# Norm 1 with common roots and weights spread by TensorE, the first projections in chunks of 256 in a fixed order, and the last pair's factors later

## The chip, the core and the metric

The kernel runs on one core of one Trainium2 chip. The metric is device time in microseconds (us) from one execution of the program to its end; the median of several runs is compared. Engines are named as the profile names them: PE is TensorE (PEld its weight loads), DVE is VectorE, ACT is ScalarE, POOL is GpSimd, SP is SyncE, which here only issues DMAs.

## What is computed

One inference step of a hybrid decoder layer for 1024 new tokens of one sequence and 8 sample tokens, 1032 rows in all, of width 1024, in fp32:

```python
h = rms_norm(x, norm1_g)                       # x * rsqrt(mean(x*x) + eps) * g
q_a, k_a, v_a, q_b, k_b, v_b, o_b, i_b, f_b, g_a, g_b = split(h @ w_in)
for g in range(3):                             # windows 128, 512, 2048; dilations 1, 4, 16
    o[g], lse[g] = dilated_attention(q_a[g], k_a[g], v_a[g], bias[g])   # 8 heads of 64
a_out = sum_g(softmax_g(lse) * o)              # factors across the three groups
hm, C, n, m = mlstm(silu(conv(q_b, k_b)), v_b, i_b, f_b)
x = x + (sig(g_a) * (a_out @ w_pa) + sig(g_b) * (sig(o_b) * hm) @ w_pb) @ w_o
x = x + conv_ffn(rms_norm(x, norm2_g)); y = rms_norm(x, final_norm_g)
```

The 8 sample tokens attend to cached keys and values instead. New keys, values and states are outputs too.

## The kernel before

**Matmuls in three passes.** Every fp32 operand is split into a high part (a cast to the matmul's format) and a low part (the rest): high by high, low activation by high weight, high activation by low weight. `mm` (L207) issues for one chunk of tokens and 128 output columns 3 passes of 8 matmuls, one for each 128 of the 1024 inputs. The 1032 rows lie in three chunks, `CHUNKS` = 352, 352 and 328 columns. A weight of 128 columns comes by SP into one of 3 raw buffers (`raw_w`, L158), ACT casts the high part (`whi`, L200), DVE subtracts for the low part (`wlo`, L201), after which the raw buffer is free. Chunks go to one of 3 PSUM buffers (`pp`), which ACT or DVE empties; other PSUM results (`X`, L98) share 5 buffers. SBUF tiles of one row width come from a pool of 16 (`A`, L90).

**Norm 1.** Nine tiles of rows (`xn0` to `xn8`, the last with 8 rows). `norm1_a` (L239): ACT squares the tile and sums it into a column of `ss` (L242), DVE makes mean plus eps (L243), ACT takes the root (L244). `norm1_b`: DVE inverts, does one Newton step (L249 to L252) and scales the tile by root and weights, `gbc`, the 1024 weights that a DMA spread over all partitions (L253). `norm1_c`: PE transposes the tile in 8 pieces into two PSUM tiles (`pxt`, L262), ACT casts the high part `act_hi` (L265). `norm1_d`: DVE subtracts for `act_lo` (L271). The loop at L289 pipelines these by one tile and splits the first three weights (query, key, value of the first unit) after tiles 1, 2 and 3. These ACT and DVE instructions are kept in the order of the program (`in_order`); PE's place is left to a scheduler. The work for the tables follows: `e4` (L300), `gT` (L306), the bias products `pv` (L317) with their copies to DRAM (`vec_d`, `rep_d`), from which POOL later loads the bias tiles `bt`.

**Units.** Each of 4 pairs of heads by 3 groups is a unit. Unit 0 is computed alone (L1013): for each chunk its query, key and value are projected (L383 ff.), and then come the key and value transposes, `ptr` (L411). From there `weave` (L938) runs a unit's attention between the projections of the next one: at step i it advances the generators that a dictionary names for i, then projects one chunk. `Ahead` (L178) loads and splits the weights before they are needed.

**The last pair.** After unit 11 a last weave (L1035) does six gate chunks (`gate_steps`, which write `tga_d`) and in between three generators of pair 3. `cb` (`combine_b`) makes the factors across groups on DVE (`fw` L586 to L598, `ff` L601), transposes them on PE (`pst`, L604) and writes `f_d` (L607). `cc` (`combine_c`) loads for each group the spread factors `fbc` (L618) and the outputs `ob` (L619) on POOL, multiplies (L628), adds (L633) and writes `aT_d`. `sa` (`sample_steps`) is the sample attention: the new rows `sn` go to DRAM (`sn_d`) and come back spread (`qb`, POOL), DVE multiplies and sums with cached keys `kt` (L671, L672), PE transposes these scores (`psc`, L688) behind a bias product (`psb`, L683); SP loads cached values `vt` (L680); then come the softmax (L693 to L697), the values' products (`pos`, L721), the output `asT` (L731) and its write. After the weave `conv_in` (L1059 to L1076) follows for column blocks of the mLSTM: a projection, its evacuation to `u` on ACT (L1063), the conv on DVE (`z`, L1071 and L1073), a tanh on ACT (L1075).

**Queues.** Each engine does its instructions in the order in which they stand, and SP and POOL issue their DMAs so too: one that waits holds those behind it.

## Time and profile before

| | us |
|---|---|
| median of 3 runs (2298.34 to 2299.7) | 2298.75 |
| the profiled execution | 2297.91 |
| its span from first to last instruction | 2295.9 |
| TensorE busy in it | 2260.7 |
| VectorE busy | 1152.2 |
| ScalarE busy | 688.4 |

Rows below come from the profiled execution, with times from the start of its span; 2.0 us lie around the span. Busy time of TensorE is a model of pipelined instructions; the start of the next group is the better mark of a group's end. The thing to read in a timeline's row is, beside its start, the bracket: how long the engine was idle before it, and what ended that.

### The profile page before, as it was taken

What the parts mean: (1) busy time and instruction counts of PE and PEld (TensorE: products, weight loads), DVE (VectorE), ACT (ScalarE), POOL (GpSimd) and SP (SyncE); (2) the same over time, 40 slices, a digit from 0 to 9 for tenths busy, and PEclk for the clock granted to TensorE, in tenths of its full rate; (3) what the DMA queues carried; (4) which work ended last, traced back from release to release, by engine and by line L of the source; (5) the groups of instructions that cost most, each with busy time, mean ns of one, the idle gap of its engine ahead of it and who ended that gap; (6) DMA issues with size and microseconds to landing.
All of it is one profiled execution on the core that took longest, in us unless ns stands there. A gap on an engine that the chain in (4) does not pass through costs nothing.

```text
span 2295.9 us, 36432 instructions
## 1 busy us (share of the span) xinstructions
PE 2260.7 (98%) x15077; PEld 2170.6 (95%) x15077; DVE 1152.2 (50%) x2680; ACT 688.4 (30%) x1346; POOL 224.5 (10%) x404
## 2 busy tenths in 40 slices
PE   6999999999989999999999999999999999999998
PEld 6899999999989999999999999999999999999997
DVE  6243544444354545556332444446655656655666
ACT  4233343343323333333222311332222222221222
POOL 1112121121220111111122100000000000000000
PEclk8999999999999999999999999999999999999999
DMA  5324453545571232414245521221111111111112
GB/s 179 98 67 116 118 122 109 143 120 136 139 229 52 80 104 67 132 57 124 79 127 173 172 60 47 79 74 56 56 38 47 46 38 56 56 55 38 47 38 78
DMA packets 246471, 209.38 MB, mean 91 GB/s; under 512 B 24777, under 2 KB 220473, under 8 KB 246290
## 3 DMA queue, kind: packets, MB, share of 16 engines
q1 hardware_dynamic: 206577, 124.65, 18.8%
q0 software_dynamic: 39728, 82.42, 11.9%
q8 instruction: 118, 1.93, 0.4%
q14 instruction: 48, 0.39, 0.1%
HBM read 166.59 MB, written 45.50 MB: 92 GB/s over the span
## 4 chain that ended last, share of the span: by engine, by line
PE 95%; DVE 1%; issue 1%; DMA 1%; ACT 1%; SPq 0%; POOL 0%; DVEq 0%; ACTq 0%; POOLq 0%
PE pp L213 71%; PE ppd L1553 11%; PE s L481 2%; PE pt L508 1%; PE po L535 1%; PE pcm L1170 1%; PE ni L1164 1%; PE ptr L411 1%; PE na L1167 1%; PE sm L1151 1%; PE pxo L1421 1%; SPq L102 0%; PE pkm L1140 0%; DMA xn<-in_x_prompt_dram 0%; PE pn L1274 0%
## 5 line engine op out<-in xcount | busy, mean ns | idle before, releaser
L213 PE MATMUL pp<-act_hi,whi 128*128 128x352 f32 (+1 forms) x3272 | 600.1, 324 | 2.3 <-ACT act_hi L265 2.0
L213 PE MATMUL pp<-act_lo,whi 128*128 128x352 f32 (+1 forms) x3272 | 582.0, 320 | 0.0
L213 PE MATMUL pp<-act_hi,wlo 128*128 128x352 f32 (+1 forms) x3272 | 579.6, 319 | 0.0
L213 PEld LDWEIGHTS pp<-act_hi,whi 128*128 128x128 f32 x3272 | 524.1, 188 | 13.2 <-issue 6.3
L213 PEld LDWEIGHTS pp<-act_lo,whi 128*128 128x128 f32 x3272 | 526.1, 187 | 1.6
L213 PEld LDWEIGHTS pp<-act_hi,wlo 128*128 128x128 f32 x3272 | 525.4, 187 | 1.6
L201 DVE TENSOR_TENSOR wlo<-wraw,whi 128x1024 fp32r<-128x1024 f32 (+2 forms) x153 | 181.9, 1189 | 370.4 <-PE pp L213 206.0
L200 ACT CAST whi<-wraw 128x1024 fp32r<-128x1024 f32 (+2 forms) x153 | 156.5, 1023 | 512.1 <-PE pp L213 457.4
L1554 DVE TENSOR_TENSOR x<-x,ppd 128x352 f32<-128x352 f32 (+4 forms) x248 | 124.6, 515 | 72.4 <-PE ppd L1553 72.3
L1479 DVE TENSOR_TENSOR fu<-pp,sq 128x320 f32<-128x320 f32 (+1 forms) x130 | 64.6, 511 | 182.2 <-PE pp L213 181.9
L1553 PE MATMUL ppd<-fhi,dhi 128*128 128x352 f32 (+3 forms) x528 | 123.7, 320 | 0.2
L1553 PE MATMUL ppd<-fhi,dlo 128*128 128x352 f32 (+3 forms) x528 | 123.9, 320 | 0.0
L1553 PE MATMUL ppd<-flo,dhi 128*128 128x352 f32 (+3 forms) x528 | 123.3, 319 | 0.0
L1493 DVE SCALAR_TENSOR_TENSOR y<-fu,fcv,y 128x1048 f32<-128x1048 f32 x88 | 115.1, 1307 | 2.4 <-ACT y L1491 1.2
L495 ACT ACTIVATE sb<-sb,st 128x128 f32<-128x128 f32 (+1 forms) x192 | 84.2, 440 | 41.0 <-DVE st L490 41.0
L1553 PEld LDWEIGHTS ppd<-fhi,dhi 128*128 128x128 f32 x528 | 89.5, 188 | 1.9 <-issue 0.5
L1553 PEld LDWEIGHTS ppd<-fhi,dlo 128*128 128x128 f32 x528 | 89.5, 188 | 1.4
L1553 PEld LDWEIGHTS ppd<-flo,dhi 128*128 128x128 f32 x528 | 89.5, 188 | 1.4
L105 POOL DMA_DIRECT2D gfin<-in_final_norm_g_dram x1 | 0.5, 527 | 912.8 <-DVE fu L1479 912.8
L374 DVE COPY vT<-pp 128x352 f32<-128x352 f32 (+1 forms) x36 | 18.5, 513 | 111.3 <-PE pp L213 111.3
L490 DVE CUSTOM_DVE_ANT_0 sb<-s,bt 128x128 f32<-128x128 f32 (+1 forms) x192 | 55.5, 348 | 29.5 <-PE s L481 23.6
L1491 ACT ACTIVATE y<-fu,fcv 128x1048 f32<-128x1048 f32 x44 | 55.7, 1266 | 30.6 <-DVE fu L1481 30.3
(382 smaller groups left out, 2319.4 us busy)
## 6 DMA issues: line engine op xcount, KB each, us to landing
wraw<-in_w_in_dram SPq DMA_DIRECT2D x84, 512.0 KB
wraw<-in_w_up_dram SPq DMA_DIRECT2D x44, 512.0 KB
draw<-in_w_down_dram SPq DMA_DIRECT2D x22, 512.0 KB
c<-in_state_mlstm_C_dram SPq DMA_DIRECT2D x32, 256.0 KB
out_dram<-c POOLq DMA_DIRECT2D x32, 256.0 KB, 3.4
o_d<-oT POOLq DMA_DIRECT2D x12, 512.0 KB, 6.5
kt<-in_cache_kv_w_dram SPq DMA_DIRECT2D x12, 512.0 KB
qb<-sn_d POOLq DMA_DIRECT2D x12, 512.0 KB, 4.7
```

What stands on the lines that cost most here:

```text
L200: a = nc.scalar.copy(hi[:, 0:n], raw[:, 0:n])
L201: b = nc.vector.tensor_tensor(out=lo[:, 0:n], in0=raw[:, 0:n], in1=hi[:, 0:n].bitcast(F32), op=ALU.subtract)
L213: nc.tensor.matmul(ps[0:m, 0:n], wt[:, i * m:(i + 1) * m], act[i][which][:, t0:t0 + n], start=(pi == 0 and i == 0), stop=(pi == 2 and i == ...
L411: nc.tensor.transpose(pt[:, i * 128:(i + 1) * 128], src[:, b * 128:(b + 1) * 128], ident)
L481: yield nc.tensor.matmul(ss_[hd][:, at[b]:at[b] + kw], qT[pr, b * 128:(b + 1) * 128], kT[pr, k0 * 128:k0 * 128 + kw], start=True, stop=True)
L490: red = nc.vector.tensor_tensor_reduce(out=sb[:, 0:kw], in0=ss_[hd][:, at[b]:at[b] + kw], in1=bias[hd][:, 256 - kw:256], scale=1.0, scalar ...
L495: in_order(nc.scalar.activation(out=sb[:, 0:kw], in_=sb[:, 0:kw], func=ACTF.Exp, scale=-1.0, bias=st[:, cm:cm + 1], accum_out=st[:, cl:cl ...
L1479: nc.vector.tensor_tensor(out=u[:, 2 + t0:2 + t0 + npm], in0=ps[:, 0:npm], in1=r2[:, t0:t0 + npm], op=ALU.mult)
L1491: nc.scalar.activation(out=y, in_=u[:, 0:YW], func=ACTF.Identity, scale=fcv3[:, 0, j:j + 1], bias=fcv3[:, 3, j:j + 1])
L1493: nc.vector.scalar_tensor_tensor(out=y, in0=u[:, i:i + YW], scalar=fcv3[:, i, j:j + 1], in1=y, op0=ALU.mult, op1=ALU.add)
L1553: nc.tensor.matmul(ps[:, 0:n], wds[j][w][:, m * 128:(m + 1) * 128], parts[j][a][:, t0:t0 + n], start=(x == 0), stop=(x == len(seq) - 1))
L1554: nc.vector.tensor_tensor(out=x1[m][:, t0:t0 + n], in0=x1[m][:, t0:t0 + n], in1=ps[:, 0:n], op=ALU.add)
```

## The change

- `gbc` is no longer spread by a DMA. A row of 1024 weights is loaded (`grow`), and PE multiplies a column of ones by it, twice 512 columns in fp32 (`pgb`); ACT copies the results to `gbc`.
- Norm 1 is cut into `squares` (ACT), `stats` (root and Newton step for a list of tiles at once, in columns of `ss`), `scale` (DVE), `turn` (PE transposes and ACT casts) and `rest` (DVE low parts). Roots are taken for tiles 0, 1, (2, 3), (4, 5) and (6, 7, 8).
- Unit 0 goes by `FIRST`, chunks of 256, 256, 256 and 264. Its matmuls and the transposes are kept in program order, and the program interleaves them: `next(u0)` projects one of query, key and value of one chunk; transposes, scalings and weight splits stand between.
- The tables' work (`e4`, `gT`, bias products, `rbx`) moves to a function `tables`, called after the key projection of the third chunk. The load of the second weight moves ahead of `xn4`.
- In the last weave the steps of `sa`, `cb` and `cc` get other places: `cb` ends at step 5, all of `cc` comes after the weave.

```diff
+FIRST = ((0, 256), (256, 256), (512, 256), (768, 264))
-    gbc = A("gbc")
-    dma_w(gbc[:, 0:DM], _bcast(norm1_g, 0, [[0, 128], [1, DM]]))
+    grow = A("grow")
+    dma_w(grow[0:1, 0:DM], norm1_g[0:1, :])
...
+    gbc = A("gbc")
+    for k0 in (0, 512):
+        pgb = X("pgb")
+        in_order(nc.tensor.matmul(pgb, ones[0:1, :], grow[0:1, k0:k0 + 512], start=True, stop=True))
+        nc.scalar.copy(gbc[:, k0:k0 + 512], pgb)
...
+    def stats(tiles):
+
+        c = slice(tiles[0], tiles[-1] + 1)
+        v, r, t = (ss[:, k + c.start:k + c.stop] for k in (16, 25, 34))
+        o(nc.vector.tensor_scalar(out=v, in0=ss[:, c], scalar1=1.0 / DM, scalar2=EPS, op0=ALU.mult, op1=ALU.add))
         o(nc.scalar.activation(out=t, in_=v, func=ACTF.Sqrt))
...
     raws = [raw_w(w_in2[:, 0:128])]
     load_x(3)
+    raws.append(raw_w(w_in2[:, AQ:AQ + 128]))
     load_x(4)
-    raws.append(raw_w(w_in2[:, AQ:AQ + 128]))
     raws.append(raw_w(w_in2[:, 2 * AQ:2 * AQ + 128]))
...
+    squares(0)
+    stats((0,))
+    squares(1)
+    scale(0)
+    turn(0)
+    stats((1,))
+    squares(2)
+    scale(1)
+    rest(0)
+    turn(1)
+    squares(3)
+    first_split()
+    rest(1)
+    stats((2, 3))
+    scale(2)
...
-                for ci in range(len(CHUNKS)):
+                for ci in range(len(FIRST)):
                     for k in range(3):
-                        proj_chunk(first_w[k], hT, evacs[k], ci)
+                        proj_chunk(first_w[k], hT, evacs[k], ci, chunks=FIRST, pin=True)
                         yield
...
-    for _ in units[0].steps():
+
+    u0 = units[0].steps()
+    next(u0)
+    turn(2)
+    scale(3)
+    rest(2)
+    first_split()
+    next(u0)
+    turn(3)
+    squares(4)
+    squares(5)
+    rest(3)
+    stats((4, 5))
+    scale(4)
+    first_split()
+    next(u0)
+    turn(4)
+    scale(5)
+    rest(4)
+    next(u0)
+    turn(5)
+    for i in (6, 7, 8):
+        squares(i)
+    rest(5)
+    stats((6, 7, 8))
+    scale(6)
+    next(u0)
+    turn(6)
...
+    next(u0)
+    e4, gT = tables()
+    for _ in u0:
...
     weave(None, gate_steps(tga_d, (2, 3)), 6, {
-        0: (sa, cb, sa, sa), 1: (cb, sa), 2: (cb, sa), 3: (cb, sa, sa), 4: (sa, cc), 5: (sa, sa, cc),
+        0: (cb, sa, sa), 1: (sa,), 2: (sa,), 3: (cb, sa), 4: (cb, sa, sa), 5: (cb, sa, sa),
```

How the rows of an engine move is shown at two places. The first is ScalarE in the head. In these rows `junk,ss<-xn` is a square, `rst<-rst` or `ss<-ss` a root, `act_hi<-pxt` the casts of a transposed tile, `whi<-wraw` the cast of a weight and `qT<-pp` or `kT<-pp` the evacuation of a projection. Before:

```order
L242 ACTIVATE junk_110,ss<-xn_101 128x1024
L244 ACTIVATE rst<-rst 128x1
L242 ACTIVATE junk_111,ss<-xn_106 128x1024
L244 ACTIVATE rst<-rst 128x1
L265 CAST act_hi<-pxt 128x4x128 x2
L242 ACTIVATE junk_110,ss<-xn_108 128x1024
L244 ACTIVATE rst<-rst 128x1
L265 CAST act_hi<-pxt 128x4x128 x2
L200 CAST whi<-wraw 128x1024
L242 ACTIVATE junk_111,ss<-xn_123 128x1024
L244 ACTIVATE rst<-rst 128x1
L265 CAST act_hi<-pxt 128x4x128 x2
```

Now, ScalarE from its first copy:

```order
L152 COPY gbc<-pgb 128x512 x2
L250 ACTIVATE junk_117,ss<-xn_101 128x1024
L259 ACTIVATE ss<-ss 128x1
L250 ACTIVATE junk_118,ss<-xn_106 128x1024
L288 CAST act_hi<-pxt 128x4x128 x2
L259 ACTIVATE ss<-ss 128x1
L250 ACTIVATE junk_117,ss<-xn_108 128x1024
L288 CAST act_hi<-pxt 128x4x128 x2
L250 ACTIVATE junk_118,ss<-xn_121 128x1024
L207 CAST whi<-wraw 128x1024
L259 ACTIVATE ss<-ss 128x2
L403 ACTIVATE qT<-pp 128x256
```

The copies of the spread weights stand first, the second root (`ss<-ss` after the first `act_hi` row) stands behind the casts of tile 0 instead of ahead of them, and the first weight's cast stands behind the square of tile 3. Further on, ScalarE around the casts of the key's and the value's weights, before:

```order
L200 CAST whi<-wraw 128x1024
L242 ACTIVATE junk_110,ss<-xn_125 128x1024
L244 ACTIVATE rst<-rst 128x1
L265 CAST act_hi<-pxt 128x4x128 x2
L200 CAST whi<-wraw 128x1024
L242 ACTIVATE junk_111,ss<-xn_131 128x1024
```

Now:

```order
L288 CAST act_hi<-pxt 128x4x128 x2
L207 CAST whi<-wraw 128x1024
L405 COPY kT<-pp 128x256
L288 CAST act_hi<-pxt 128x4x128 x2
L250 ACTIVATE junk_117,ss<-xn_125 128x1024
L250 ACTIVATE junk_118,ss<-xn_129 128x1024
L259 ACTIVATE ss<-ss 128x2
L207 CAST whi<-wraw 128x1024
L288 CAST act_hi<-pxt 128x4x128 x2
```

The value's weight, the last `whi` row, now stands behind two squares and their common root, which themselves stand behind the casts of tile 3 and the evacuation of the first key chunk.

The second place is the last weave, on TensorE: `pst` is the factors' transpose, `psb` and `psc` belong to the sample scores. Before:

```order
L213 MATMUL pp<-act_hi,whi 128x352 x8
L213 MATMUL pp<-act_lo,whi 128x352 x7
L604 MATMUL pst<-ident,ff 48x128
L683 MATMUL psb<-ohs,rbx 16x129 x3
L688 MATMUL psc<-ident,sc 16x128
L213 MATMUL pp<-act_lo,whi 128x352
L213 MATMUL pp<-act_hi,wlo 128x352 x8
L688 MATMUL psc<-ident,sc 16x128
```

Now:

```order
L220 MATMUL pp<-act_hi,whi 128x352 x8
L220 MATMUL pp<-act_lo,whi 128x352 x8
L220 MATMUL pp<-act_hi,wlo 128x352 x8
L716 MATMUL psb<-ohs,rbx 16x129 x3
L721 MATMUL psc<-ident,sc 16x128 x2
L220 MATMUL pp<-act_hi,whi 128x352 x8
L220 MATMUL pp<-act_lo,whi 128x352 x7
L721 MATMUL psc<-ident,sc 16x128
L723 MATMUL psc<-ones,qk_207 16x1 x3
L220 MATMUL pp<-act_lo,whi 128x352
L220 MATMUL pp<-act_hi,wlo 128x352 x8
L637 MATMUL pst<-ident,ff 48x128
```

The factors' transpose moved from ahead of the scores to behind them and 24 matmuls. On POOL at this place, from the write of the factors, before:

```order
L108 DMA f_d_404<-fr 48x128
L105 DMA fbc<-f_d_404 128x1x1024
L105 DMA ob<-o_d_0_419 128x1024
L105 DMA fbc<-f_d_404 128x1x1024
L105 DMA ob<-o_d_1_420 128x1024
L105 DMA fbc<-f_d_404 128x1x1024
L105 DMA ob<-o_d_2_421 128x1024
L108 DMA tga_d<-tga 128x1032
L108 DMA aT_d<-asT 128x8
```

Now:

```order
L109 DMA f_d_219<-fr 48x128
L106 DMA fbc<-f_d_219 128x1x1024
L109 DMA tga_d<-tga 128x1032
L106 DMA ob<-o_d_0_234 128x1024
L106 DMA fbc<-f_d_219 128x1x1024
L109 DMA aT_d<-asT 128x8
L106 DMA ob<-o_d_1_235 128x1024
L106 DMA fbc<-f_d_219 128x1x1024
L106 DMA ob<-o_d_2_236 128x1024
```

A gate write and the write of the sample output, `aT_d<-asT`, now stand between the loads of factors and outputs. On SP one weight load of the three that stood behind the cached values (`vt`) stands ahead of them.

## Rows read from the trace of the kernel before

**Rows 1.** The page, part 1 (busy us and share of the span of each engine) and the first line of part 4 (shares of the chain that ended last).
```profile
PE 2260.7 (98%) x15077; PEld 2170.6 (95%) x15077; DVE 1152.2 (50%) x2680; ACT 688.4 (30%) x1346; POOL 224.5 (10%) x404
...
PE 95%; DVE 1%; issue 1%; DMA 1%; ACT 1%; SPq 0%; POOL 0%; DVEq 0%; ACTq 0%; POOLq 0%
```

**Rows 2.** Timeline of TensorE (PE) in the head; columns: start us, us, engine, line, operation, out<-in, shapes, count, and in brackets the idle time before it and what ended it. `pxt` are transposed tiles, `pp` projections, `pv` the bias products, `ptr` the key and value transposes of the first unit.
```profile
9.76 1.97 PE L262 MATMUL pxt<-ident,xn 128*128 128x128 f32 x8 [9.76 <-DVE rst L243]
...
19.12 3.01 PE L213 MATMUL pp<-act_hi,whi 128*128 128x352 f32 x9 [2.01 <-ACT act_hi L265]
...
32.20 1.03 PE L262 MATMUL pxt<-ident,xn 128*128 128x128 f32 x8
32.99 1.52 PE L213 MATMUL pp<-act_lo,whi 128*128 128x352 f32 x8
...
42.37 4.00 PE L317 MATMUL pv<-oh,rb 33*8 33x384 f32 x6
46.30 2.71 PE L213 MATMUL pp<-act_hi,whi 128*128 128x352 f32 x8
48.81 2.55 PE L213 MATMUL pp<-act_lo,whi 128*128 128x352 f32 x8
...
60.17 1.36 PE L213 MATMUL pp<-act_hi,whi 128*128 128x328 f32 x8
...
70.94 0.71 PE L411 MATMUL ptr<-ident,vT 128*128 128x128 f32 x5
```

**Rows 3.** Waits of TensorE from 0 to 72 us: who waits, for whom, us in total, times, longest us.
```profile
PE pxt L262 <- DVE xn L253: 6.1, 4, 2.5
PE pp L213 <- ACT act_hi L265: 2.0, 1, 2.0
```

**Rows 4.** Table by stretches; columns: from:to, us, busy us and instructions of PE, PEld, DVE, ACT and POOL, the granted clock of TensorE, DMA share, GB/s. One stretch of the head, one of the second place.
```profile
40.00:50.00 10.00, 8.66 (x28) 5.36 (x29) 4.99 (x11) 1.13 (x5) 3.69 (x5) 0.55 0.14 35
...
645.00:652.00 7.00, 4.96 (x19) 3.92 (x20) 6.52 (x10) 0.92 (x3) 2.08 (x4) 0.51 0.47 154
```

**Rows 5.** Timeline of TensorE in the second place: the factors' transpose, and the first and the third `conv_in` projection.
```profile
647.04 0.38 PE L604 MATMUL pst<-ident,ff 128*48 128x128 f32 x1 [5.97 <-DVE ff L601]
...
662.90 0.76 PE L213 MATMUL pp<-act_hi,whi 128*128 128x352 f32 x3
...
685.79 1.46 PE L213 MATMUL pp<-act_hi,whi 128*128 128x352 f32 x8
```

**Rows 6.** Timeline of TensorE in the last output projection, where matmuls have 256 columns.
```profile
2273.18 0.63 PE L1553 MATMUL ppd<-fhi,dlo 128*128 128x256 f32 x4
2273.65 0.64 PE L1553 MATMUL ppd<-fhi,dhi 128*128 128x256 f32 x4
```

**Rows 7.** Timeline of ScalarE (ACT) in the head: the first square, the second root, the first cast of a transposed tile, the first cast of a weight.
```profile
4.19 1.06 ACT L242 ACTIVATE junk<-xn 128x1024 f32<-128x1024 f32 x1 [1.96 <-DMA xn<-in_x_prompt_dram]
...
9.80 0.20 ACT L244 ACTIVATE rst<-rst 128x1 f32<-128x1 f32 x1 [0.24 <-DVE rst L243]
10.91 0.58 ACT L265 CAST act_hi<-pxt 128x512 fp32r<-128x512 f32 x1 [0.90 <-PE pxt L262]
...
14.66 1.06 ACT L200 CAST whi<-wraw 128x1024 fp32r<-128x1024 f32 x1
```

**Rows 8.** Timeline of VectorE (DVE) in the head: the scaling of tiles 0 and 1.
```profile
8.41 1.28 DVE L253 SCALAR_TENSOR_TENSOR xn<-xn,rst,gbc 128x1024 f32<-128x1024 f32 x1
...
10.87 1.28 DVE L253 SCALAR_TENSOR_TENSOR xn<-xn,rst,gbc 128x1024 f32<-128x1024 f32 x1
```

**Rows 9.** The tile view of `rep_d`, 40 to 120 us: its DMA issues (durations ns min/median/max, first and last start us), and their time from issue to landing.
```profile
L108 POOL DMA_DIRECT2D rep_d<-vec_d x4: 1087/1106/1116, 47.9 to 51.1; - x4
...
DMA to landing us min/median/max: 2.3/4.0/19.5
```

**Rows 10.** Timeline of VectorE: the first reader of the bias tables.
```profile
97.66 0.28 DVE L490 CUSTOM_DVE_ANT_0 sb<-s,bt 128x128 f32<-128x128 f32 x1
```

**Rows 11.** Timeline of VectorE in the second place: the low part of a weight, the first product of sample queries and cached keys, and the last product of outputs and factors.
```profile
632.71 1.22 DVE L201 TENSOR_TENSOR wlo<-wraw,whi 128x1024 fp32r<-128x1024 f32 x1 [5.01 <-ACT whi L200]
...
642.30 1.23 DVE L671 TENSOR_TENSOR qb<-qb,kt 128x1024 f32<-128x1024 f32 x1 [7.69 <-DMA qb<-sn_d]
...
675.56 1.23 DVE L628 TENSOR_TENSOR ob<-ob,fbc 128x1024 f32<-128x1024 f32 x1 [0.70 <-DMA ob<-o_d]
```

**Rows 12.** Timeline of SP's queue there: cached values (`vt`), then weights.
```profile
623.31 8.08 SPq L102 DMA_DIRECT2D vt<-in_cache_kv_w_dram  x3
633.96 28.51 SPq L102 DMA_DIRECT2D wraw<-in_w_in_dram  x3
```

**Rows 13.** The tile view of `sn` over the whole run (one write for each of the four pairs).
```profile
DMA to landing us min/median/max: 1.8/2.2/8.3
```

**Rows 14.** Timeline of POOL there: the write of the sample rows, the loads of the queries, the last load of a group's outputs.
```profile
628.57 0.57 POOL L108 DMA_DIRECT2D sn_d<-sn  x1
637.11 1.07 POOL L105 DMA_DIRECT2D qb<-sn_d  x2 [7.97 <-DMA sn_d<-sn]
...
653.98 0.57 POOL L105 DMA_DIRECT2D ob<-o_d  x1
```

**Rows 15.** Timeline of ScalarE there: the first two evacuations of the second `conv_in` projection.
```profile
685.21 0.79 ACT L1063 COPY u<-pp 128x352 f32<-128x352 f32 x2
```

**Rows 16.** The tile view of `ob`, 620 to 680 us: time of its DMAs from issue to landing.
```profile
DMA to landing us min/median/max: 3.6/16.8/21.5
```

122 lines of the change are left out of this document (66 added, 56 removed).

## The prediction

> **What bounds the kernel now.** I began with the page: TensorE is busy for 2260.7 of 2295.9 us, and the chain that ended last is TensorE for 95% [rows 1]. So an edit counts by what it does to TensorE's idle time, to the clock it is granted, or to its number of cycles; work of the other engines counts only where TensorE waits for it. The diff and the order of the instructions show two places that change: the head, up to the first key transposes, and the last pair's samples and factors near 640 us. For both I then read the timelines.
>
> In the head, TensorE starts at 9.76 and reaches the key transposes at 70.94 [rows 2], 61.2 us later. Its waits in between are 6.1 us for scaled tiles, in four waits, and 2.0 for a cast, together 8.1 us [rows 3]. How much of the rest is work at full clock? Chunk 3 of the first three projections (72 matmuls of 328 columns) takes 60.17 to 70.94, 10.77 us [rows 2], so 0.150 us each and by columns 0.160 for 352: 3.86 us for 24 of these, 23.2 for six chunks. Eight transposes at speed take 32.20 to 32.99, 0.79 us, nine tiles 7.1. The bias products took 4.00 us in a stretch at a granted clock of 0.55 [rows 2, 4], so 2.0 at full. Sum 43.1. The remainder, 61.2 - 8.1 - 43.1 = 10.0 us, is half clock, 1.2 GHz: the first transposes (1.97 instead of 0.79), the bias products, eight matmuls in 2.51 instead of 1.28 at 46.30 [rows 2].
>
> In the second place TensorE waits 5.97 us for the factors, until 647.04 [rows 5], and then runs at a granted clock of 0.51 until 652 [rows 4], where half of 4.96 busy us is lost, 2.5. Together 8.5 us: the most that this place can give.
>
> **The change, the head.** *Columns.* Nine chunks of 256 and three of 264 replace nine of 352 and 328. Four 256-column matmuls take 2273.18 to 2273.65 [rows 6], 0.1175 each; 9x24x0.1175 + 3x24x0.121 = 34.1 against 34.0 us. Cost 0.1 to 0.3; I take 0.3.
>
> *Start.* Before, the first square began at 4.19 [rows 7] and the scaling at 8.41 [rows 8]. Now ScalarE's first work is two copies of the spread weights, in front of that square. They wait for a 4 KB row (behind the first tile on SP, so I estimate 4.5) and two fp32 products of 512 columns. The three of 384 took 4.00 us at about half clock [rows 2, 4], so these take 2 x 1.78. With the copy (near 0.58, as the cast from PSUM [rows 7]) the square begins near 8.7. From there 1.2 for the square, 0.2 for the VectorE step, then 1.07 from root to scaling (9.80 to 10.87 [rows 7, 8]): scaling at 11.2, first transposes 1.35 later as before, 12.5. That is +2.8 us. The broadcast load that goes, 512 KB, had its cover: the scaling waited for the square of its own tile too.
>
> *Order of ScalarE.* This is the larger term. ScalarE keeps its order, so whatever stands behind a cast of transposes waits for TensorE. Tile by tile, with casts of 0.58 a half, squares of 1.2, 1.06 for a weight split and 1.28 for a scaling [rows 7, 8]:
> - Root 1 now stands behind tile 0's casts (before it stood ahead, 9.80 against 10.91 [rows 7]). Transposes 12.5 to 14.3 at half clock, casts until 14.9, root, 1.07 to the scaling at 16.0, 1.3 to the transposes at 17.3: TensorE idles 3.1.
> - The first weight split stands behind tile 1's casts and square 3: 19.0 + 0.7 + 1.2 + 1.06 = 22.0 for the first projection, idle 3.0 (before 19.12 [rows 2]). Its second pass waits 0.7 for the second low part of tile 1, which VectorE does after that weight's.
> - The key's split stands behind tile 2's casts, whose transposes stand behind all of the first projection on TensorE: idle 1.8 (a cast, then 1.06).
> - The value's split stands behind tile 3's casts, squares 4 and 5 and their common root: 0.7 + 2.4 + 0.4 + 1.06 = idle 4.6.
> - Tile 6 is scaled after one root for 6 to 8, whose three squares stand behind tile 5's casts: 3.5 for the squares, 1.6 for the root's steps, 1.3 for the first scaling, less the 2 us of key projection that covers: idle 4.3.
>
> Sum 3.1 + 3.0 + 0.7 + 1.8 + 4.6 + 4.3 = 17.5 against 8.1: +9.4. The batched roots save VectorE work (some four sets of small steps), but VectorE isn't what these steps wait for.
>
> *Clock.* The half-clock loss was 10.0. I keep it: the start is as cold, and the bias products no longer follow a 2.5 us wait, but there are five gaps of 2 to 5 us. Bounds: 5 us less, if the clock rises soon after 22 and stays; 12 more, if it stays low until the last gap.
>
> The Trainium skill, "TensorE: Matmul & The Clock Gate", section "HAM oscillation — how this bites in real kernels", describes a kernel whose waits between bursts return the clock to half each time. This trace agrees once: the 5.97 us wait is followed by 7 us near 0.51 [rows 4, 5]. By that rule the new gaps would cost more than the 10.0 that I keep, the sum being then that of rival 1 below.
>
> Head: 2.8 + 9.4 + 0.3 = **+12.5** (+7 to +24). The tables are now written 26 us later (products end at 72 instead of 46.3). Their slowest copy took 19.5 us from its issue at 51.1 in the worst case [rows 9], so no later than 71, and 97 now, with the load of the biases about 101; its reader, at 97.66 [rows 10], itself moves to about 110. Free, with 9 us of cover.
>
> **The change, the second place.** One weight load now stands ahead of the three cached-value loads on SP. It waits for a raw buffer that is read until 633.9 [rows 11], so the value loads leave 623 to 631 [rows 12], where they met the write of the sample rows (8.3 us to landing; of the four pairs the least was 1.8, the median 2.2 [rows 13]). With 2.2 to 3 the row is there near 631.7 rather than 636.9, the query loads 5.2 later (637.11 to 642.30 [rows 11, 14]) near 637. Score products come ahead of the factors' transpose on TensorE, which moves 24 matmuls back. So the 6 us idle time should largely go: TensorE gets to the first conv projection some 7.9 us earlier than 662.90 [rows 5] (8.5, less a 0.6 us wait for the third score).
>
> But what is late next? Before, the third conv projection began at 685.79 [rows 5] on a PSUM buffer whose reader is the u copy of 685.21 on ScalarE [rows 15], behind a tanh that ends a VectorE run which began with the last product of outputs and factors, 675.56, released by the load of these outputs [rows 11]. 685.21 + 0.46 = 685.67 against 685.79: no slack. The gain of 7.9 us is kept only if that load lands earlier. It will not: the factors' transpose is later on TensorE (648.5 instead of 647.04), and POOL now does a gate write and the sample output's write between the loads; the latter waits for the samples' last products, about 656. I place the last load's issue at 658.9 instead of 653.98 [rows 14]. The loads took 3.6 to 21.5 us, median 16.8 [rows 16]; from 658.9 that is 675.7 to 680.4 and I take 678. So the third projection starts 2.5 to 3 us later than before, after about 10 us of idle time, which brings half clock as the 6 us did: 2.5 again. **+5.5**, bounds -1 and +10.
>
> **Sum.** 2297.91 + 12.5 + 5.5 = 2315.9 by the profiled run, 2295.9 its span plus 2.0 around it. The median of the runs is 0.8 above it, so 2316 to 2317; I say **2316**. A measurement of this kernel can tell about 0.2%, 4.6 us.
>
> **Rivals.**
> 1. *Low clock through the head.* If every gap returns the clock to 1.2 GHz until tile 6's, the work from 12.5 to 58 runs at half: some 22 us of full-clock work, so 22 lost instead of 10: 2328. For it: 0.51 after one wait of 6 us [rows 4]. Against: before, the clock rose despite waits of 2 us. Chance 0.10. The section of the Trainium skill named above, in "TensorE: Matmul & The Clock Gate", speaks for this rival.
> 2. *Late queries.* The value loads, started at 634, meet the query loads instead of the sample write. If they land at 642.3 as before, the same wait moves from the factors to the scores, and the last outputs are later again: tail +10, 2321. Chance 0.17.
> 3. *The gain of the second place is kept*: its transfers land by their median or faster, the conv step does not bind. +12.5 - 8.5: 2303. Against: zero slack in 685.67. Chance 0.10.
> 4. *Faster: the projections cover the norm as the order has it.* From the first projection at 22 TensorE finds everything ready: 43.2 - 1.6 of work, 3 of half clock, so the key transposes at 66.6, -4.3, and with the second place between 0 and -8.5: 2286 to 2294. It decides if the weight splits at k and v are ready when TensorE is; the price of failure is the 1.8, 4.6 and 4.3 above. Against: ScalarE can't run past a cast that waits for TensorE. Chance 0.07.
>
> **How the numbers follow.** The forecast, 2308 to 2320, has 0.56; its lower part is the clock's lower bound with a flat tail. Rivals 2 and 1 lie above, 2320 to 2330; 3 near 2303, within or just over 0.2%; 4 below. Range 2302 to 2326 leaves out rival 4, half of 3 and most of 1. Faster by over 0.2%: 0.06; within: 0.08; slower: 0.86.
>
> **What would show it.** The square of tile 0 near 8.7, the first projection near 22, waits for weight splits at k and v of chunk 1 and a wait for tile 6's scaling, each 2 to 5 us; the key transposes at 80 to 86. In the second place no wait before the factors' transpose, and a wait of 8 to 12 us at the third conv projection released by ScalarE. Wrong if the key transposes start before 74, or if no wait takes the place of the 5.97 us.

## The result, and the profile after

| | before | after |
|---|---|---|
| median of 4 runs each, us | 2298.55 | 2325.73 (2324.4 to 2327.9) |
| ratio, with its 95% interval | | 1.0118 [1.0101, 1.0136] |
| the profiled execution, us | 2297.91 | 2327.0 |
| its span, us | 2295.9 | 2324.9 |

The change makes the kernel 27.2 us slower by the medians, 29.0 by the spans. The bound has not changed: on the page, TensorE's busy time is 6.9 us longer than in [rows 1] (3.75 are the spread of the weights, 2.8 the half clock found below), and the other 22 us are idle.

```profile
PE 2267.6 (98%) x15153; PEld 2176.5 (94%) x15153; DVE 1150.5 (49%) x2665; ACT 689.1 (30%) x1346; POOL 224.9 (10%) x404
```

I find the 29.0 us by three marks on TensorE's timeline. The key transposes start at 81.19 instead of 70.94, **+10.25**. The third conv projection starts at 711.81 instead of 685.79 [rows 5], which is +26.02, so **+15.8** between the two marks. Its 24 matmuls last until 718.43 at a granted clock of 0.55, 6.62 us instead of 3.86, **+2.8**. The sum is 28.8.

**The head.** TensorE's timeline, the first transposes, the instructions that waited for a scaling or a cast, and the mark (columns: start us, us, engine, line, operation, out<-in, shapes, count, and in brackets the idle time and what ended it):

```profile
12.86 1.97 PE L285 MATMUL pxt<-ident,xn 128*128 128x128 f32 x8 [4.30 <-DVE ss L258]
17.76 1.97 PE L285 MATMUL pxt<-ident,xn 128*128 128x128 f32 x8 [2.93 <-DVE xn L274]
22.39 2.07 PE L220 MATMUL pp<-act_hi,whi 128*128 128x256 f32 x8 [2.65 <-ACT whi L207]
...
30.73 1.23 PE L220 MATMUL pp<-act_hi,whi 128*128 128x256 f32 x8 [1.67 <-ACT whi L207]
...
38.91 2.08 PE L220 MATMUL pp<-act_hi,whi 128*128 128x256 f32 x8 [4.18 <-ACT whi L207]
...
54.65 1.11 PE L285 MATMUL pxt<-ident,xn 128*128 128x128 f32 x8 [3.84 <-DVE xn L274]
...
81.19 1.12 PE L444 MATMUL ptr<-ident,vT 128*128 128x128 f32 x8
```

Against [rows 2, 3]: the first transposes start 3.1 us later. Then five waits, 2.93 + 2.65 + 1.67 + 4.18 + 3.84 = 15.3 us, stand where 8.1 stood. What is left by the working of the prediction (full-clock work of 43.1 us and 0.1 more for the columns), 81.19 - 12.86 - 15.3 - 43.2 = 9.9 us, is what that working calls half clock, 10.0 before. By an estimate, 1 us of it is not: at full clock, the 24 matmuls of 256 columns between two groups of transposes take 43.98 to 46.91, 2.93 us, where [rows 6] gave 2.82, and there are nine such groups. Why TensorE waits is read from ScalarE's timeline (same columns), to be set beside [rows 7]:

```profile
15.34 0.21 ACT L259 ACTIVATE ss<-ss 128x1 f32<-128x1 f32 x1
...
18.91 0.58 ACT L288 CAST act_hi<-pxt 128x512 fp32r<-128x512 f32 x1 [2.33 <-PE pxt L285]
...
21.30 1.03 ACT L207 CAST whi<-wraw 128x1024 fp32r<-128x1024 f32 x1
...
34.33 1.07 ACT L288 CAST act_hi<-pxt 128x512 fp32r<-128x512 f32 x2
35.29 1.07 ACT L250 ACTIVATE junk<-xn 128x1024 f32<-128x1024 f32 x1
...
36.34 1.05 ACT L250 ACTIVATE junk<-xn 128x1024 f32<-128x1024 f32 x1
...
37.83 1.03 ACT L207 CAST whi<-wraw 128x1024 fp32r<-128x1024 f32 x1
```

The root of tile 1 (L259, 15.34) starts only when tile 0's casts are over, and the scaling that waits for it ends TensorE's 2.93 us. The first weight's cast (L207, 21.30) stands behind the casts of tile 1 (L288, 18.91) and a square, and ends the 2.65. The third weight's cast (37.83) stands behind the casts of tile 3 and two squares; TensorE has nothing to do until it is over, 4.18 us. The other two waits go the same way: the second weight's cast stands behind tile 2's casts (1.67), and the common root of tiles 6 to 8 (51.97) behind their three squares, which stand behind tile 5's casts (47.55), and so the scaling that ends the 3.84.

**The second place.** Here I subtract 10.25 from after's times to set them beside those of before. TensorE's timeline:

```profile
654.42 0.27 PE L721 MATMUL psc<-ident,sc 128*16 128x128 f32 x1 [0.99 <-DVE fw L619]
657.44 0.38 PE L721 MATMUL psc<-ident,sc 128*16 128x128 f32 x1 [2.75 <-DVE sc L705]
...
664.38 0.27 PE L637 MATMUL pst<-ident,ff 128*48 128x128 f32 x1
...
668.70 0.90 PE L220 MATMUL pp<-act_hi,whi 128*128 128x352 f32 x4
...
711.81 2.71 PE L220 MATMUL pp<-act_hi,whi 128*128 128x352 f32 x8 [17.65 <-ACT u L1135]
...
718.43 1.45 PE L220 MATMUL pp<-act_hi,whi 128*128 128x352 f32 x8
```

The wait of 5.97 us for the factors [rows 5] is gone (664.38 has no bracket). Instead TensorE waits 0.99 + 2.75 us for the scores (the first of these is put down to `fw`, the instruction behind the first scores on VectorE). The first conv projection starts at 668.70 - 10.25 = 658.45, 4.5 us earlier than before. Then the third one waits 17.65 us for ScalarE's copy of `u`. The chain behind that copy is followed back through the timelines of ScalarE, VectorE and POOL, the landing of `ob` (us from issue to landing, min/median/max; this view counts the write `aT_d<-ob` beside the loads) and SP's queue:

```profile
710.34 1.08 ACT L1147 ACTIVATE th<-z 128x1056 f32<-128x1056 f32 x1 [26.91 <-DVE z L1145]
711.32 0.79 ACT L1135 COPY u<-pp 128x352 f32<-128x352 f32 x2
```

```profile
651.79 1.23 DVE L704 TENSOR_TENSOR qb<-qb,kt 128x1024 f32<-128x1024 f32 x1 [7.71 <-DMA qb<-sn_d]
...
701.86 1.22 DVE L661 TENSOR_TENSOR ob<-ob,fbc 128x1024 f32<-128x1024 f32 x1 [1.11 <-DMA ob<-o_d]
```

```profile
638.19 0.53 POOL L109 DMA_DIRECT2D tga_d<-tga  x1 [2.63 <-ACT tga L920]
638.71 0.57 POOL L109 DMA_DIRECT2D sn_d<-sn  x1
644.87 1.08 POOL L106 DMA_DIRECT2D qb<-sn_d  x2 [5.59 <-DMA sn_d<-sn]
...
665.47 0.54 POOL L109 DMA_DIRECT2D f_d<-fr  x1 [11.05 <-ACT fr L639]
...
669.01 0.55 POOL L109 DMA_DIRECT2D tga_d<-tga  x1 [0.47 <-ACT tga L920]
...
673.30 0.55 POOL L109 DMA_DIRECT2D aT_d<-asT  x1 [2.38 <-DVE asT L764]
...
675.18 0.57 POOL L106 DMA_DIRECT2D ob<-o_d  x1
```

```profile
DMA to landing us min/median/max: 3.2/22.4/26.6
```

```profile
644.57 3.91 SPq L103 DMA_DIRECT2D vt<-in_cache_kv_w_dram  x3
...
670.04 12.91 SPq L103 DMA_DIRECT2D c<-in_state_mlstm_C_dram  x4
```

The copy of `u` (711.32) stands behind a tanh (710.34) that waited for VectorE's conv step, and VectorE's last product of outputs and factors (701.86) stands ahead of that step. This product waits for the last load of outputs: 675.18 + 26.6 = 701.8. That load is issued 10.9 us later than in [rows 14] (675.18 - 10.25 = 664.93 against 653.98) and takes 5.1 us longer than the slowest of [rows 16]. The two make 16.0, and the third projection is 15.8 later: nothing lies between but a chain without slack.

The least of each such landing view, 3.2 here and 3.6 in [rows 16], is that of the write `aT_d<-ob`. By the DMA view of the loads alone (out<-in, queue, count, KB each, median us from issue to landing), first before, then after:

```profile
ob<-o_d POOLq DMA_DIRECT2D x3, 512.0 KB, 19.6
```

```profile
ob<-o_d POOLq DMA_DIRECT2D x3, 512.0 KB, 24.3
```

One by one, the three loads took 16.8, 19.6 and 21.5 us before, and 20.4, 24.3 and 26.6 after.

### The profile page after: what moved, and what is told of

Its sections match the earlier page's. It is cut to its first block, busy times and chain, and to the rows that moved or that the text cites. A ratio compares the mean times of both kernels' runs of the same rounds, so it can differ in the third digit from the quotient of the medians.

```text
span 2324.9 us, 36566 instructions
## 1 busy us (share of the span) xinstructions
PE 2267.6 (98%) x15153; PEld 2176.5 (94%) x15153; DVE 1150.5 (49%) x2665; ACT 689.1 (30%) x1346; POOL 224.9 (10%) x404
## 3 DMA queue, kind: packets, MB, share of 16 engines
q1 hardware_dynamic: 206435, 124.12, 19.1%
q0 software_dynamic: 39728, 82.42, 11.7%
## 4 chain that ended last, share of the span: by engine, by line
PE 93%; DMA 2%; ACT 1%; issue 1%; DVE 1%; SPq 1%; POOL 0%; DVEq 0%; ACTq 0%; POOLq 0%
PE pp L220 70%; PE ppd L1625 10%; PE s L514 2%; PE pt L541 1%; PE po L568 1%; PE pcm L1242 1%; DMA ob<-o_d 1%; PE ni L1236 1%; PE ptr L444 1%; PE na L1239 1%; SPq L103 1%; PE sm L1223 1%; PE pxo L1493 1%; PE pkm L1212 0%; PE pn L1346 0%
## 5 line engine op out<-in xcount | busy, mean ns | idle before, releaser
L220 PE MATMUL pp<-act_hi,whi 128*128 128x352 f32 (+3 forms) x3296 | 603.9, 325 | 26.5 <-ACT u L1135 17.7
L220 PE MATMUL pp<-act_lo,whi 128*128 128x352 f32 (+3 forms) x3296 | 585.1, 320 | 0.0
L220 PE MATMUL pp<-act_hi,wlo 128*128 128x352 f32 (+3 forms) x3296 | 580.6, 318 | 0.0
L220 PEld LDWEIGHTS pp<-act_hi,whi 128*128 128x128 f32 (+1 forms) x3296 | 526.6, 189 | 37.5 <-ACT u L1135 17.9
L220 PEld LDWEIGHTS pp<-act_lo,whi 128*128 128x128 f32 (+1 forms) x3296 | 529.6, 189 | 1.7
L220 PEld LDWEIGHTS pp<-act_hi,wlo 128*128 128x128 f32 (+1 forms) x3296 | 526.5, 188 | 1.6
L207 ACT CAST whi<-wraw 128x1024 fp32r<-128x1024 f32 (+2 forms) x153 | 156.4, 1022 | 515.5 <-PE pp L220 462.2
L407 DVE COPY vT<-pp 128x352 f32<-128x352 f32 (+2 forms) x37 | 18.7, 504 | 104.9 <-PE pp L220 104.9
```

Of the source, the lines that this page charges most:

```text
L207: a = nc.scalar.copy(hi[:, 0:n], raw[:, 0:n])
L220: a = nc.tensor.matmul(ps[0:m, 0:n], wt[:, i * m:(i + 1) * m], act[i][which][:, t0:t0 + n], start=(pi == 0 and i == 0), stop=(pi == 2 and ...
```

## The experiments

My theory after the result: two independent places. In the head ScalarE's program order is the cause. In the second place the loads of outputs leave POOL too late, and land slowly since SP's loads run beside them. The rivals: in the head, the spread by TensorE or the small chunks are what costs; in the second place, POOL's own order (a gate write and the sample output's write between the loads) is all, or the lateness of the factors is all. Ratios are to the kernel before, run beside each on the same chip.

**1. The two places apart.** Both kernels change only the table of the last weave; `e1` has the changed head, `e2` the changed table:

```diff
 e1: after, with the old table
-        0: (cb, sa, sa), 1: (sa,), 2: (sa,), 3: (cb, sa), 4: (cb, sa, sa), 5: (cb, sa, sa),
+        0: (sa, cb, sa, sa), 1: (cb, sa), 2: (cb, sa), 3: (cb, sa, sa), 4: (sa, cc), 5: (sa, sa, cc),
 e2: before, with the new table (the same two lines, the other way round)
```

> The changed kernel with the old order of steps in the last weave, so the new head alone. If the two places simply add up, as the traces say (key transposes at 81.19 instead of 70.94), it costs 10.3 us: 2309. Rival: the later head also shifts the transfers of the last pair against each other, and a part of the 18.6 us lost there remains: 2312 or more. Third: the head's loss is made good later: 2299.

> The kernel before with the new order of steps in the last weave only. Theory: this place alone loses 15.8 us at the third conv projection plus 2.7 of half clock, so 2317. If the order itself were harmless and only its meeting with the later head cost: near 2299.

Measured: `e1` 2310.38 us, 1.0051 [1.0036, 1.0066], +12.0; `e2` 2312.49, 1.0061 [1.0046, 1.0076], +14.2. The sum, 26.2, is nearly the whole 27.2, so the places add up within the intervals. `e2` comes out below the 2317 expected. In `e2`, on TensorE's timeline, the wait has moved as in after; the landing of `ob` beside it:

```profile
698.53 2.72 PE L213 MATMUL pp<-act_hi,whi 128*128 128x352 f32 x8 [18.07 <-ACT u L1063]
```

```profile
DMA to landing us min/median/max: 3.2/21.9/27.0
```

The third conv projection is 12.7 us later than before: the last load is issued 7.5 later (661.47) and lands 5.5 slower (27.0 against 21.5), 13.0 together. This is the same reckoning as in after, in another kernel.

**2. The head: one root earlier.** `e5` is `e1` with the root of tile 1 ahead of tile 0's transposes and casts:

```diff
     scale(0)
-    turn(0)
     stats((1,))
+    turn(0)
     squares(2)
```

> As the changed kernel with the old weave, but the root of tile 1 stands ahead of the casts of tile 0 on ScalarE again, nothing else. Theory (ScalarE's order holds the head): the wait of 2.93 us before tile 1's transposes falls to about 0.5, but the first projection waits for the weight's cast behind tile 1's casts and square 3, which come 2 to 2.5 us earlier: 2 to 2.5 us less than the new head with the old weave. Rival (the weights, loaded later, or the clock hold it): no change, the wait at the first projection grows by the same.

Measured: 2307.92 us, 1.0041 [1.0026, 1.0055], 2.5 less than `e1`. The wait before tile 1's transposes falls from 2.93 to 0.49 us; the waits of 2.65, 1.67, 4.18 and 3.83 stay, and one of 0.54 is new. Only this root changes its place, so one instruction's place in ScalarE's order is one wait of TensorE, as the theory has it.

**3. The head: ScalarE's whole order.** `e6` keeps the spread, the chunks of 256 and the order on TensorE, and has the old table. VectorE's scalings and the weights' low parts change their places with the casts. Roots, squares and weight casts, which need nothing from TensorE, come ahead of the casts that wait for it; the weight's cast and its low part are called apart (`first_hi`, `first_lo`):

```diff
     scale(0)
-    turn(0)
     stats((1,))
     squares(2)
+    turn(0)
     scale(1)
     rest(0)
+    first_hi()
     turn(1)
     squares(3)
-    first_split()
     rest(1)
+    first_lo()
     stats((2, 3))
+    first_hi()
+    squares(4)
+    squares(5)
     scale(2)
+    first_lo()
+    scale(3)
...
     next(u0)
     turn(2)
-    scale(3)
     rest(2)
-    first_split()
+    first_hi()
+    first_lo()
+    stats((4, 5))
+    scale(4)
     next(u0)
+    for i in (6, 7, 8):
+        squares(i)
     turn(3)
...
```

> The new head with the old weave, with ScalarE's order changed alone: the second root, the squares and the three weight casts stand ahead of casts that wait for TensorE; the order on TensorE, the chunks, the spread weights and the common roots stay. Theory (ScalarE's order makes the waits of 2.9, 2.7, 1.7, 4.2 and 3.8 us): these fall to 4 us in all, and the half clock with them; key transposes at 67 to 71, 2295 to 2299. Rival (chunks of 256 leave TensorE short of tiles, whatever ScalarE does, since VectorE is the bound): the waits move to scaled tiles, 2305 or more.

Measured: 2290.75 us, 0.9962 [0.9947, 0.9977]: 19.6 less than `e1`, 8 less than before, and below what I expected. TensorE's timeline, its waits and the mark, then ScalarE's:

```profile
12.28 1.97 PE L285 MATMUL pxt<-ident,xn 128*128 128x128 f32 x8 [4.30 <-DVE xn L274]
14.73 1.80 PE L285 MATMUL pxt<-ident,xn 128*128 128x128 f32 x8 [0.49 <-DVE xn L274]
...
19.06 1.23 PE L220 MATMUL pp<-act_hi,wlo 128*128 128x256 f32 x8 [0.17 <-DVE wlo L321]
21.69 1.09 PE L285 MATMUL pxt<-ident,xn 128*128 128x128 f32 x8 [1.40 <-DVE xn L274]
...
29.64 1.06 PE L285 MATMUL pxt<-ident,xn 128*128 128x128 f32 x8 [0.28 <-DVE xn L274]
...
62.22 1.12 PE L466 MATMUL ptr<-ident,vT 128*128 128x128 f32 x8
```

```profile
12.32 0.20 ACT L259 ACTIVATE ss<-ss 128x1 f32<-128x1 f32 x1 [1.21 <-DVE ss L258]
...
13.47 0.56 ACT L288 CAST act_hi<-pxt 128x512 fp32r<-128x512 f32 x1
...
14.76 1.05 ACT L312 CAST whi<-wraw 128x1024 fp32r<-128x1024 f32 x1
...
19.23 1.03 ACT L312 CAST whi<-wraw 128x1024 fp32r<-128x1024 f32 x1
...
23.46 1.06 ACT L312 CAST whi<-wraw 128x1024 fp32r<-128x1024 f32 x1
```

On ScalarE the second root (12.32) now precedes the first cast of a transposed tile (13.47), and the weights are cast from 14.76, 19.23 and 23.46 instead of 21.30, 29.62 and 37.83. TensorE's waits are 0.49 + 0.17 + 1.40 + 0.28 = 2.3 us instead of 15.3. The rest, 62.22 - 12.28 - 2.3 - 43.2, leaves 4.4 us; in `e1` it was 82.95 - 12.03 - 15.3 - 43.2 = 12.4. So of the 20.7 us that the mark moved, 13 are waits and 8 what this working calls half clock, of which 2 to 3 may be chance (below). The rival that the spread or the small chunks are what costs falls: both are still there. What the changed order on VectorE gives of this, `e6` doesn't tell apart; in after's rows the waits follow ScalarE, and `e5` moves ScalarE alone.

**4. The head: spread and chunk size by themselves.** `e12` is `e1`, `e7` is `e6`, both with `gbc` loaded by a DMA as before; `e10` is `e7` with chunks of 352, 352 and 328 instead of four small ones:

```diff
 e7 and e12
-    grow = A("grow")
-    dma_w(grow[0:1, 0:DM], norm1_g[0:1, :])
+    gbc = A("gbc")
+    dma_w(gbc[:, 0:DM], _bcast(norm1_g, 0, [[0, 128], [1, DM]]))
...
 e10, beside that
-                for ci in range(len(FIRST)):
+                for ci in range(len(CHUNKS)):
-                        proj_chunk(first_w[k], hT, evacs[k], ci, chunks=FIRST, pin=True)
+                        proj_chunk(first_w[k], hT, evacs[k], ci, pin=True)
...
     u0 = units[0].steps()
-    next(u0)
     turn(2)
```

> As the last one (new ScalarE order, old weave), but the norm's weights come by the broadcast DMA again, without the products and copies. Theory (the spreading costs the 3.1 us of the later start): 2 to 3 us less than with the products. Rival (the half megabyte delays the tiles and weights behind it by its 1.4 us, and these now set the pace): less than 1 us less, or more.

> The changed kernel's head with the old weave, where only the spreading is undone: the norm's weights come by the broadcast DMA again, ScalarE's order and all else stay. Theory (the later start, 3.1 us, is carried through a head that is bound by ScalarE's order): 2.5 to 3.5 us less than the same with the spreading (2310.4). Rival (later waits take it up, since they are for loads of tiles and weights that now come 1.4 us later): less than 1.5.

> The best head so far with the old chunks of 352, 352 and 328 in the first unit, in a fixed order too; old weave. It tells what the chunk size itself does. If the order on ScalarE is all that mattered, the first projection waits for one more tile (2 to 3 us) and the rest follows without waits: 2290 to 2293. If the smaller chunks are what lets TensorE run without waits: 2296 or more.

Measured: `e12` 2306.76 us, 1.0032 [1.0022, 1.0043], 3.6 less than `e1` by the medians and 4.3 by what each has over its own before; `e7` 2289.28, 0.9954 [0.9940, 0.9969], 1.5 less than `e6`, which the intervals don't tell apart; `e10` 2293.43, 0.9977 [0.9968, 0.9986], 4.1 more than `e7` and near the case in which the order matters most. The first transposes start at 7.98 in `e12` and 8.20 in `e7`, some 4 us earlier than with the spread. Where ScalarE's order binds, nearly all of that reaches the end; where it doesn't, 2.4 us reach the mark (59.81 against 62.22), since what is left for half clock is 1.4 more (59.81 - 8.20 - 2.6 - 43.2 = 5.8 against 4.4), a difference that may be chance. In `e10` the waits are 1.85 + 5.16 + 0.46 + 0.24 = 7.7 us against 2.6, and the mark is 4.85 later: a chunk of 352 needs a third tile before it can start. The small chunks gain.

**5. The second place: what slows the loads.** `e3` is after with SP's weight loads from the end of the last weave on, and the loads of the states, pinned to their place in the program, so that SP starts them behind the outputs:

```diff
+        if late:
+            in_order(d)
...
+    late.append(1)
...
-            dma_w(c0.rearrange("p (f v) -> p f v", f=2), st_C[0, b, self.h].rearrange("(f p) v -> p f v", p=128))
+            in_order(nc.sync.dma_start(out=c0.rearrange("p (f v) -> p f v", f=2), in_=st_C[0, b, self.h].rearrange("(f p) v -> p f v", p=128)))
```

> The changed kernel, in which SP issues the loads of the mLSTM states behind the weights of the following projections instead of in the middle of the loads of factors and outputs. Theory: the outputs' last load took 26.6 us instead of 21.5 because it met these state loads; without them 17 to 20 us, the third conv projection 6 to 9 us earlier, 2317 to 2320. Rival: its delay is all in the issue on POOL, the transfers are as slow alone: 2325.

Measured: 2346.94 us, 1.0205 [1.0188, 1.0222]. The total, far from the 2317 to 2320 expected, says nothing on the question, since the pinned weights themselves came late: TensorE waits 19.43 us for a `wlo` at 693.37. The landing does. The table by stretches (from:to, busy us and instructions of PE, PEld, DVE, ACT, POOL, the granted clock, DMA share, GB/s), first of after, then of `e3`, and the landing of `ob` in `e3`:

```profile
680.00:695.00 15.00, 14.16 (x92) 13.89 (x90) 1.33 (x3) 1.55 (x3) 0.00 (x0) 1.00 0.88 216
```

```profile
680.00:695.00 15.00, 1.63 (x5) 1.63 (x6) 6.60 (x8) 0.00 (x0) 0.00 (x0) 0.50 0.27 91
```

```profile
DMA to landing us min/median/max: 3.5/17.1/18.7
```

With the DMA engines at a share of 0.27 instead of 0.88 the same three loads, issued within 1.4 us of the same time, land after 18.7, 17.1 and 17.4 us instead of 20.4, 24.3 and 26.6, and the row that they end in is written to `aT_d` at 697.02 instead of 704.64. So some 9 us of the last load's landing is contention with SP's loads; whether weights or states weigh more, this edit doesn't tell. The Trainium skill, "DMA: Bandwidth & Descriptors", section "Issuing engines are not separate DMA queues", says that DMAs of different engines run on the same 16 DMA engines and interleave; these rows agree.

**6. The second place: POOL's order.** `e8` is after with all six loads of factors and outputs on POOL directly behind the factors' write:

```diff
-        0: (cb, sa, sa), 1: (sa,), 2: (sa,), 3: (cb, sa), 4: (cb, sa, sa), 5: (cb, sa, sa),
+        0: (cb, sa, sa), 1: (sa,), 2: (sa,), 3: (cb, sa), 4: (cb, sa, sa), 5: (cb, cc, cc, sa, sa),
...
         load(1)
+        if pair == 3:
+            load(2)
         yield
...
-                load(2)
+                if pair < 3:
+                    load(2)
```

> The changed kernel, in which POOL issues the six loads of the last factors and outputs right behind the factors' write, ahead of a gate write and of the write of the sample output; the rest of the order stays. Theory: of the 11 us by which the last load was issued later, 3 to 4 are POOL's wait for the sample output: the last load near 671.5 instead of 675.2, 3 to 4 us less: 2322. Rival (the state loads make the transfers late, whenever they are issued): unchanged, 2326.

Measured: 2319.57 us, 1.0089 [1.0074, 1.0104], 6.2 less than after. TensorE's wait, and the landing of `ob`:

```profile
705.82 2.72 PE L220 MATMUL pp<-act_hi,whi 128*128 128x352 f32 x8 [11.45 <-ACT u L1138]
```

```profile
DMA to landing us min/median/max: 3.3/19.3/24.2
```

The key transposes are at 82.66 here, 11.7 later than before, so the third conv projection is 705.82 - 11.7 - 685.79 = 8.3 us later than before, where after had 15.8. The last load is issued 5.7 later (671.44 - 11.7 - 653.98) and lands 2.7 slower, 8.4 together. From the factors' write to the last load POOL takes 5.8 us here, 9.7 in after: 3.9 of the 7.5 gained are its order itself. The factors' write comes 1.3 earlier and the landing is 2.4 shorter; whether these two follow from the order, the run doesn't tell. What is left is the factors' write, 5.9 later than before, and the landing. Neither rival is all of it.

**7. The second place: everything early.** `e4` is before with the factors ahead of the scores and pinned gate projections. `e9` is `e7` with all three query loads first, then the factors and all six loads, and the scores pinned behind the gate chunks. `e11` is `e9` with the cached values loaded directly behind the cached keys:

The tables of `e4` and of `e9` and `e11`:

```diff
-        0: (sa, cb, sa, sa), 1: (cb, sa), 2: (cb, sa), 3: (cb, sa, sa), 4: (sa, cc), 5: (sa, sa, cc),
+        0: (sa, cb, cb, sa), 1: (cb, sa), 2: (cb, cc, sa), 3: (cc, sa), 4: (sa,),
...
-        0: (cb, sa, sa), 1: (sa,), 2: (sa,), 3: (cb, sa), 4: (cb, sa, sa), 5: (cb, sa, sa),
+        0: (sa, cb, cb, sa), 1: (cb, sa), 2: (cb, cc, cc, sa), 3: (sa,), 4: (sa,),
```

In `e9`, `load(2)` stands with `load(1)` for the last pair, in the sample steps and in `combine_c`. In `e11`, for the last pair, the loop that loads `vt` has moved from behind the scores:

```diff
+        def load_v():
+            for g in range(3):
+                vts.append(A("vt", 1024))
...
+            load_v()
...
-        vts = []
-        for g in range(3):
-            vts.append(A("vt", 1024))
...
+        if pair < 3:
+            load_v()
```

> The kernel before with another order in its last weave: the factors' steps all ahead of the sample scores, the scores' transposes held behind the four gate chunks that are left, the loads of factors and outputs right behind the factors. Theory (the third conv projection follows the last load of outputs by 10.2 us, and TensorE's wait of 5.97 us was a wait for the queries, handed on through VectorE's order): no wait at the factors, none over 2 us at the scores, the last load of outputs issued 3 to 5 us earlier, 4 to 8 us less: 2290 to 2294. Rival: the transfers, not their issue, set the end there, and the loads now meet those of the queries: same time as before or up to 5 us more.

> The best head so far (new ScalarE order, weights by DMA) with a last weave in which all query loads stand ahead of the factors on POOL, the factors ahead of the scores on VectorE and TensorE, the six loads right behind the factors, and the scores' transposes behind the four gate chunks that are left. Theory (the third conv projection stands 10.2 us behind the last load of outputs): no wait at factors or scores over 2 us, the last load issued some 8 us earlier and landing in 20 to 25 us: 4 to 8 us less than the same head with the old weave (2289.3), so 2281 to 2285. Rival (the transfers of queries, values, factors and outputs share one bandwidth, and an earlier issue only lengthens them, as in the run where the factors went first): 2288 to 2300, with a wait for the scores.

> As the run with both (best head; queries, factors, loads, then scores), but SP issues the three cached-value loads right behind the keys, ahead of the weights. Theory (the 17.1 us wait for these values was an order on SP, not bandwidth): no wait over 3 us left in the second place; 2281 to 2286. Rival (all transfers share one bandwidth, so what comes earlier makes another later): a wait of 5 us or more at queries or values, 2289 or more.

Measured: `e4` 2310.00 us, 1.0046 [1.0029, 1.0063]; `e9` 2299.12, 1.0000 [0.9991, 1.0010]; `e11` 2285.52, 0.9940 [0.9927, 0.9954]. The first two miss what was expected (2290 to 2294, and 2281 to 2285), the third has it. In `e4` the third load of queries stands behind loads of factors and outputs on POOL; the landing of `qb`, and TensorE's wait for the scores:

```profile
DMA to landing us min/median/max: 5.0/5.6/23.4
```

```profile
668.47 0.38 PE L690 MATMUL psc<-ident,sc 128*16 128x128 f32 x1 [17.85 <-DVE sc L674]
```

In `e9` scores and factors are in time, and TensorE waits for the cached values, 11.85 us and then 5.00 and 0.24 more. Their loads stand on SP behind two weights, and SP takes 19.20 us to start them:

```profile
656.44 1.08 PE L775 MATMUL pos<-vt,pz 128*32 128x128 f32 x16 [11.85 <-DMA vt<-in_cache_kv_w_dram]
```

```profile
633.18 19.20 SPq L103 DMA_DIRECT2D vt<-in_cache_kv_w_dram  x3
```

In `e11` SP starts these loads at 612.72, and one wait is left there, for a weight:

```profile
634.67 2.71 PE L214 MATMUL pp<-act_hi,wlo 128*128 128x352 f32 x8 [4.62 <-DVE wlo L202]
```

So the 5.97 us of before were one of a row of waits: factors, then scores, then values, then a weight, each with its own issue time. Moving one group earlier on a shared queue only passes the wait on. `e11`, with all of them set, beats both kernels: 13.5 us below before, of which 9.5 are the head's (`e7`) and 3.9 this place's.

## Why the forecast was right, and where it was off

The forecast was 2316, slower, for two reasons. The sign was right, and both places lose by the mechanism that was named: ScalarE's order, and a late last load with no slack behind it. That 2325.73 lies inside the range is luck: it is 0.3 us from the range's end and outside 2308 to 2320, in the stretch that the prediction gives to its rivals 1 and 2. The head came out 2.3 us below its term, the second place 13.1 above and outside its bounds. The terms:

- **The start** (+2.8): 3.1 measured. With a DMA instead of the spread, the first transposes start at 7.98 (`e12`), 1.8 earlier than before, so the spread itself costs the start 4 us. Undoing it alone gave 3.6 us with after's order (`e12`), and 1.5 with that of `e6` (`e7`).
- **ScalarE's order** (17.5 us of waits): 15.3. The single ones were forecast as 3.1, 3.0, 0.7, 1.8, 4.6 and 4.3, and are 2.93, 2.65, none, 1.67, 4.18 and 3.84, in the same places. `e5` and `e6` show that the cause is the order. With another order it could be mended for 20 us: what rival 4 (the projections cover the norm) describes is what `e6` does.
- **The columns** (+0.3): about 1 us by the rows above, an estimate; it was taken from four matmuls of [rows 6].
- **The clock in the head** (10.0 unchanged): 9.9 by the same working, some 1 us less with the columns taken out. Rival 1, low clock through the head, didn't happen. The Trainium skill, "TensorE: Matmul & The Clock Gate", section "HAM oscillation — how this bites in real kernels", on which that rival leaned, tells of waits between bursts that return the clock to half. Single waits here agree in part (behind the one of 4.18 us eight matmuls take 2.08 us, and 1.12 from 42.23 on; behind the one of 1.67 us they take 1.23), but over the head the loss didn't grow with the waits.
- **The second place** (+5.5, bounds -1 and +10): +18.6, and here the forecast failed. The step that failed is "I place the last load's issue at 658.9 ... and I take 678". The issue came at 664.9, 6 us later, and the landing took 26.6 us instead of 19.1, 7.5 more: together 13.5, against the 13.1 by which the term was too small. Of the 7.5, 2.4 are a reading of [rows 16]: its 3.6 is the write `aT_d<-ob` and its 16.8 the first load, while the last load itself had taken 21.5. The other 5.1 are a slower landing. SP's loads of states ran beside it before too, but began 8.6 us behind the last load's issue (662.57), and in after 5.1 ahead of it (670.04); that this shift is what slowed it was not tested by itself. In `e2`, where the first product began at 638.60, near the 637 of the forecast, the last load took 27.0, so this step fails there as well. The half-clock term behind it (2.5) was right, 2.8, though the 7 us near 0.51 that the prediction sets behind the wait of 5.97 are the whole stretch of [rows 4], and 5 of them follow the wait.
- **Why the issue was late**: the premise that the sample rows would land in 2.2 to 3 us and the first product start near 637. It started at 651.79 - 10.25 = 641.5, against 642.30 before. The write of the sample rows (POOL, 638.71) took 5.9 us, though SP started the value loads no earlier than 644.57. So those loads were not the only thing that had slowed this write in [rows 13]. In the last pair it stands right behind the write of a gate, `tga_d` (638.19, 516 KB on the same queue; the sample rows are 36 KB), and the two land within 0.3 us of each other: gate and sample rows after 8.6 and 8.3 us before, 6.2 and 5.9 in after, 5.1 and 4.8 in `e2`, 2.9 and 2.7 in `e4`. The other three pairs of [rows 13] have a write of 64 KB there, and the sample rows landed after 1.8 to 2.6 us. No run tests this by itself. Then the value loads met the query loads, and the first of these took 6.9 us instead of 5.2. That is the condition of rival 2 (late queries): the wait moved to the scores, and the last outputs came later still. Its 2321 was nearer than the forecast's 2316; rival 1's 2328 was nearer yet, but what it describes didn't happen.
- **From the factors to the last load**: right. The factors' transpose, which stands behind the scores, was forecast at 648.5 and came at 664.38 - 10.25 = 654.1; from there to the last load's issue 10.4 us were forecast, and 10.8 passed (6.9 before), with the gate write (669.01) and 2.38 us of waiting for the sample output (673.30) in between. So 5.6 of the issue's 6.0 us come from the samples.
- **No slack behind that load**: right, to 0.3 us, in after, `e2` and `e8`.

Still open: what sets the landing of the gate write and the sample rows behind it, the shares of weights and states in the slow landing of the outputs, and VectorE's share in the gain of `e6`.

## What to carry to other kernels

On an engine that keeps its order, put what needs nothing from TensorE (roots, squares, weight casts) ahead of what waits for TensorE: in this head that, with VectorE's order moved along, was worth 20 us, more than chunk size or the way the norm's weights are spread. When a wait for a transfer is removed, look for the transfer that is issued behind it, and price it by issue time plus a landing with the traffic that will then run beside it, not by its landing of before. Where transfers of several consumers share a queue, set the issue order of all of them, since moving one passes the wait to the next.
